# An encoder trunk on one core: two whole tiles set among a lone pair's products, weight tiles picked by time, residual tiles reloaded by pairs, a shorter last norm and an early table load

## The chip, the cores and the metric

The kernel runs on one core of a Trainium2 chip. A core has five engines with queues of their own: TensorE (PE), which multiplies matrices; VectorE (DVE), ScalarE (ACT) and GpSimd (POOL), which work elementwise; and SyncE (SP), which here only issues transfers. Operands lie in an on-chip memory of 128 partitions; TensorE writes its sums into PSUM banks, which another engine reads out (the text calls that an evacuation). The metric is device microseconds of one execution, as a median over runs; less is better.

## The reference, cut to what matters

One layer of an encoder serves 512 prompt tokens and 64 tokens of a running stream together (T = 576 columns). All arithmetic is float32.

```
x += Mixer(RMSNorm(x))          # gated DeltaNet || gated linear attention, both in chunks, merged by sigmoids
x += CrossAttn(RMSNorm(x), mem) # 4 heads into 256 memory tokens; for the prompt, keys and values come from mem
x += ConvFFN(RMSNorm(x))        # up 1024 -> 2 x 2816, causal conv of width 3, SiLU gate, down 2816 -> 1024
y  = RMSNorm(x)                 # norm_final
```

Outputs are y for all tokens, the new recurrent and convolution states, and the memory's keys and values.

## The kernel before

**Layout.** Activations lie with features on partitions: x is eight tiles x[0..7] of 128 features by 576 tokens. A weight tile is 128x1024: eight blocks of 128x128 for one output tile. Every float32 factor is split into a high part in the type float32r (fp32r in the rows) and a low part, the rest; a product is three matmuls, high x high, high x low, low x high. `proj` (L694) does so for a whole output tile in one two-bank PSUM tile (`big`, two of them); for most weights it comes with all low-weight matmuls last (`late`).

**Products by pairs.** Many weights are taken two output tiles at a time (a pair) by a scheme of seven half-size products, P1, Q5, Q6, P2, P3, Q7 and Q4, in place of eight (`products`, L1495; the order is `product_order`, L91). P1, Q6, Q7 and Q4 of a pair add up in one bank in turn ("a"), and each is read out by DVE (the `finish` functions) before the next may add to it. The operands are sums and differences of activation halves (`operands`, L1472: tu, tw, ach, acl and hl in the profile), made by DVE, ACT and POOL ahead of time, and of weight quarters (`emit_product`, L552: ws).

**Weights.** `emit_weight` (L521) loads a float32 tile by SP into a raw tile (wr), makes the high part and the negated raw on ACT, and adds the raw once more into the negated part by an accumulating transfer, issued by POOL: that gives the low part ("w<-wt" and "w<-ws" among the transfers). Some kinds use DVE or POOL instead. Raw tiles come from a ring of 3, high and low tiles from one of 6 (`raw_tile` L506, `w_tile` L513). Half way, `swap_pools` (L1522) gives the space of the small tiles of the recurrent part to a second pool, fp: one more raw tile (rawf), three more w tiles (wf), and eight tiles F0 to F7. Of such a tile the driver knows that it is free at `drv.swapped`, the time of the small tiles' last use. `raw_tile` and `w_tile` take the new ring's tile while that ring isn't full, or where it is free sooner. `fetch` (L620) emits weights ahead in the order of `weight_order` (L64) as long as w tiles are left.

**The order of the work.** A driver (L212) plans while the program is built. `main` (L1534) yields at every few matmuls; between them side chains (spawned generators) are advanced whose inputs the plan holds for ready. Each instruction gets a planned start from cost constants, and each engine's queue is written in the order of planned starts. On the chip every engine takes its queue in that order and waits by semaphores. TensorE's own order is the program's.

**The stages the change touches.**
- Start: 18 warm-up matmuls on a tile of ones (L636) while the first x tiles and weight parts arrive by SP; then high and low parts of x (`xprep`), and the first two projections.
- From the projections to the mixer's output: gate tiles, pool swap, four `out` tiles, the gate pairs' products, `mem_prep` (L2091: loads the memory tiles and makes their high and low parts mh and ml, all at one place), four more `out` tiles. There all eight x tiles are loaded again into F0 to F7 at once (L1753). Then keys and values of the memory, and the four w_o pairs (`wo_finish` adds to x).
- Down projection: partial sums over four parts of the inner features (`ffn_order`, L116). Of part 2, the last pair, tiles 6 and 7, is left over and done alone after the last up projection. It is followed by two whole tiles (0 and 1) of part 3 without the last activation, which is added when it is ready, by the pairs (2, 3) and (4, 5), and by tiles 6 and 7 in halves of the tokens.
- Last norm (L1969 on): acc holds the squares of tiles 0 to 5, sq those of tiles 6 and 7. `sums` adds the three over the features for 128 tokens with a matmul each; `roots` takes the power -0.5; `flip` turns the tiles to tokens on partitions; `put_out` scales and stores them.

```
seq.append(("dns", [(("dn", (6, 2)), ("dn", (7, 2)))]))                  # L126, the lone pair
return seq + [("dn", (0, 1)), ("dns", ...(2, 4)), ("dn", (6, 7))]        # L127
if fp is not None and (len(drv.ring.get("rawf", ())) < RF or drv.free_at("rawf") < drv.free_at("raw")):   # L507
for i, src in enumerate([acc] + sqs[t < 2]):                             # L1999, sums
```

All instructions are recorded by one helper, so every row of the profile has line 244; the tiles' names tell them apart.

## Time and profile before

| | us |
|---|---|
| median of 3 runs | 1117.86 |
| lowest, highest | 1116.87, 1120.01 |
| the profiled execution | 1115.69 |
| its span, first to last instruction | 1113.9 |
| PE busy | 1095.8 |
| DVE busy | 719.3 |
| ACT busy | 660.2 |
| POOL busy | 309.7 |

The rows of the profile read as follows. A timeline row has the start in us from the span's beginning, the time from the group's first start to its last end, the engine (PEld is TensorE's load of the stationary factor; a q stands for an engine's queue that issues transfers), the operation, the tile written, the tiles read, the shape and the count; in brackets stands the idle time of the engine before it and what ended it. Instructions of a kind are merged in such rows, also over others between them. A row of waits has the total, the number and the longest. A row of the table of stages has the stretch, its length, the busy time of PE, PEld, DVE, ACT and POOL with counts, the granted clock, the share of busy transfer engines and GB/s. A row of the chain that ended last has start, length and what the end hung on. The row "DMA to landing" belongs to a tile's transfers in a stretch: least, median and longest time from issue to landing. Ends of matmuls are modelled, so I reckon PE by starts.

### The profile page before, as it was taken

Reading aid. Unit: us, or ns where it says so; the run is one execution under the profiler, and the core shown is the slowest. Engines: PE = TensorE matmul, PEld = TensorE weight load, DVE = VectorE, ACT = ScalarE, POOL = GpSimd, SP = SyncE. Lnnn points to the kernel's source line nnn. Section 1 sums busy time; section 2 is a strip of 40 time slices with the busy share of each in tenths; the row PEclk is TensorE's granted clock in tenths of the full one; section 3 lists DMA queues with packets and bytes.
Section 4 is the critical chain, followed back from the end, with each engine's and each line's share of the span. In section 5 each row is a group of like instructions: output and inputs, shape, how many; then the busy total and the mean of one; then the engine's idle time right before and its main releaser. Section 6 shows DMA issues by size and latency. Waiting matters only on the chain.

```text
span 1113.9 us, 21561 instructions
## 1 busy us (share of the span) xinstructions
PE 1095.8 (98%) x8331; PEld 1058.1 (95%) x8331; DVE 719.3 (65%) x1475; ACT 660.2 (59%) x1254; POOL 309.7 (28%) x559
## 2 busy tenths in 40 slices
PE   9999999999999999999999999999999999999997
PEld 8999989998998999989999999999999999999997
DVE  5566854864654766877557677567836783766585
ACT  6665645563754468466646666665646564656455
POOL 0243315230431233131210122323423242324242
PEclk9999999999999999999999999999999999999999
DMA  8566542453454769797764737975897579749644
GB/s 282 132 151 152 117 79 77 81 120 100 120 121 112 173 157 213 253 229 194 192 169 112 182 79 162 227 168 111 169 231 183 107 166 240 185 92 209 151 98 119
DMA packets 65158, 173.05 MB, mean 155 GB/s; under 512 B 7584, under 2 KB 20000, under 8 KB 65056
## 3 DMA queue, kind: packets, MB, share of 16 engines
q0 software_dynamic: 28368, 72.89, 38.1%
q1 hardware_dynamic: 36688, 98.79, 26.5%
q8 instruction: 66, 1.08, 0.4%
q14 instruction: 36, 0.29, 0.1%
HBM read 161.03 MB, written 5.37 MB: 149 GB/s over the span
## 4 chain that ended last, share of the span: by engine, by line
PE 94%; DMA 2%; DVE 2%; ACT 1%; issue 1%; SPq 0%; ACTq 0%; DVEq 0%
PE big L244 60%; PE sm L244 34%; DMA wr<-wt 1%; DMA w<-wt 1%; DMA w<-ws 1%; ACT w L244 1%; DVE w L244 0%; DVE x L244 0%; DMA x<-xT 0%; DVE ml L244 0%; DVE acl L244 0%; DVE gt L244 0%; DVE acc L244 0%; ACT vraw L244 0%; ACT kgt L244 0%
## 5 line engine op out<-in xcount | busy, mean ns | idle before, releaser
L244 PE MATMUL big<-xh,w 128*128 128x256 f32 (+1 forms) x2816 | 508.9, 300 | 1.5 <-ACT w L244 1.4
L244 PEld LDWEIGHTS big<-xh,w 128*128 128x128 f32 x2816 | 423.8, 189 | 6.5 <-issue 2.0
L244 PE MATMUL big<-xl,w 128*128 128x256 f32 (+1 forms) x1408 | 301.4, 295 | 0.0
L244 PEld LDWEIGHTS big<-xl,w 128*128 128x128 f32 x1408 | 236.8, 189 | 0.2 <-DVE xl L244 0.2
L244 POOL DMA_DIRECT2D w<-wt x129 | 113.2, 880 | 375.5 <-ACT w L244 304.9
L244 PE MATMUL sm<-ach,w 128*128 128x288 f32 (+2 forms) x1008 | 207.0, 296 | 4.2 <-DVE x L244 3.8
L244 ACT CAST w<-wr 128x1024 fp32r<-128x1024 f32 (+3 forms) x195 | 161.5, 830 | 20.9 <-PE big L244 10.1
L244 ACT ACTIVATE w<-wr 128x1024 fp32r<-128x1024 f32 (+3 forms) x174 | 145.2, 835 | 45.4 <-PE big L244 27.4
L244 PEld LDWEIGHTS sm<-ach,w 128*128 128x128 f32 x1008 | 163.6, 188 | 6.3 <-DVE x L244 2.4
L244 PE MATMUL sm<-acl,w 128*128 128x288 f32 (+2 forms) x504 | 138.0, 295 | 0.0
L244 PEld LDWEIGHTS sm<-acl,w 128*128 128x128 f32 x504 | 94.8, 188 | 0.0
L244 DVE TENSOR_TENSOR fu<-big,rbc 128x512 f32<-128x512 f32 (+1 forms) x88 | 36.4, 453 | 77.5 <-PE big L244 75.1
L244 DVE SCALAR_TENSOR_TENSOR fc<-fu,vec,fc 128x578 f32<-128x578 f32 x88 | 72.3, 824 | 20.8 <-ACT fc L244 19.8
L244 ACT ACTIVATE fc<-fu,vec 128x578 f32<-128x578 f32 x44 | 38.4, 872 | 78.4 <-DVE fu L244 78.4
L244 ACT CAST w<-ws 128x384 fp32r<-128x384 f32 (+2 forms) x100 | 53.1, 547 | 34.8 <-DVE ws L244 25.0
L244 POOL COPY fout<-fu 128x2 f32<-128x2 f32 x88 | 29.8, 382 | 151.2 <-DVE fu L244 151.2
L244 DVE TENSOR_TENSOR x<-x,sm 128x288 f32<-128x288 f32 (+2 forms) x127 | 54.1, 440 | 25.7 <-PE sm L244 25.3
L244 DVE TENSOR_TENSOR w<-ws,w 128x384 fp32r<-128x384 f32 (+2 forms) x75 | 46.2, 621 | 14.1 <-ACT w L244 12.9
L244 POOL DMA_DIRECT2D w<-wd x45 | 39.7, 888 | 48.7 <-ACT w L244 45.7
L244 PE MATMUL big<-oh,w 128*128 128x256 f32 (+1 forms) x256 | 45.2, 296 | 3.6 <-DMA w<-wt 2.4
L244 PEld LDWEIGHTS big<-oh,w 128*128 128x128 f32 x256 | 38.6, 188 | 4.2 <-DMA w<-wt 2.6
L244 DVE SCALAR_TENSOR_TENSOR c<-u,vec,c 128x579 f32<-128x579 f32 x36 | 29.4, 820 | 2.6 <-ACT c L244 1.8
(361 smaller groups left out, 1762.3 us busy)
## 6 DMA issues: line engine op xcount, KB each, us to landing
wr<-wt SPq DMA_DIRECT2D x134, 512.0 KB, 6.1
w<-wt POOLq DMA_DIRECT2D x96, 512.0 KB, 7.2
wr<-wd SPq DMA_DIRECT2D x24, 384.0 KB, 5.9
w<-wt POOLq DMA_DIRECT2D x33, 256.0 KB, 6.3
w<-wd POOLq DMA_DIRECT2D x36, 192.0 KB, 5.5
x<-xT SPq DMA_DIRECT2D x16, 288.0 KB, 6.0
w<-ws POOLq DMA_DIRECT2D x11, 256.0 KB, 5.0
w<-ws POOLq DMA_DIRECT2D x12, 192.0 KB, 4.7
```

What stands on the lines that cost most here:

```text
L244: fn(*args, **kw)
```

## The change

Six edits come together.
- **Mix.** The two whole tiles 0 and 1 of part 3 no longer follow the lone pair's seven products but stand among them: after the third product the first part of tile 0 (three activations, in the order 18, 19, 20), after the fourth its low-weight part, after the fifth and sixth the same of tile 1, then the seventh product. The last activation's part follows as before.
- **Tile by time.** `first` compares when the next tile of either ring is free, with `drv.swapped` for one not yet taken, instead of taking the new ring first.
- **Residual tiles by pairs.** x[0] and x[1] are loaded again at the first memory values, the next two after P1 of each w_o pair.
- **Memory tiles as a chain.** `c_mem_prep` issues all four loads and then prepares one tile at a time, spaced by 1.5 us of planned time.
- **Table load.** A tanh on 16 columns of the ones tile stands at the very start; mhalf is set after it. The warm-up has 20 matmuls instead of 18.
- **Last norm.** The squares of tile 6 are added into acc on DVE, so that `sums` has two operands instead of three; tokens 512 to 575 are turned into a `big` tile and tokens 0 to 255 into `sm` tiles, the other way round than before.

```diff
--- before.py
+++ after.py
@@ -35,7 +35,7 @@
 HOP = 0.2
 BACK = 6.0
 MARGIN = 0.6
-NWARM = 18
+NWARM = 20


 C_GMIX, C_GKV, C_GMEM, C_GFFN, C_GFIN = 0, 8, 16, 24, 32
@@ -74,11 +74,15 @@
         else:
             seq += [(kd, (4 if kd == "mv" else 2) * i + j) for j in range(4 if kd == "mv" else 2)]
     seq += [("mo", 0), ("mo", 1)] + [("*", u) for u in product_order(MPAIRS, True)]
-    for kd, i in FFN:
+    for kd, i, *mixed in FFN:
         if kd == "up":
             seq += [("up", i), ("up", NJ + i)]
         elif kd == "dns":
             seq += [("*", u) for u in product_order(i)]
+        elif kd == "mix":
+
+            of_pair = [("*", u) for u in product_order(mixed[0])]
+            seq += of_pair[:3] + [("dn", (i[0], 3))] + of_pair[3:5] + [("dn", (i[1], 3))] + of_pair[5:]
         else:
             seq += [("dn", (m, 3)) for m in i]
     return seq
@@ -122,9 +126,7 @@
             late = []
         pairs = [(("dn", (m, p)), ("dn", (m + 1, p))) for m in range(0, 8, 2)]
         late = [("dns", pairs if p < 2 else pairs[:3])]
-        if p == 3:
-            seq.append(("dns", [(("dn", (6, 2)), ("dn", (7, 2)))]))
-    return seq + [("dn", (0, 1)), ("dns", [(("dn", (m, 3)), ("dn", (m + 1, 3))) for m in (2, 4)]), ("dn", (6, 7))]
+    return seq + [("mix", (0, 1), [(("dn", (6, 2)), ("dn", (7, 2)))]), ("dns", [(("dn", (m, 3)), ("dn", (m + 1, 3))) for m in (2, 4)]), ("dn", (6, 7))]


 FFN = ffn_order()
@@ -285,6 +287,11 @@
         q.append(n)
         self.fresh.add(n)
         return tile_
+
+    def first(self, tag, bufs, other, n):
+
+        free = [(self.swapped if t in ("rawf", "wf") else 0.0) if len(self.ring.get(t, ())) < k else self.free_at(t)[0] for t, k in ((tag, bufs), (other, n))]
+        return free[0] < free[1]

     def free_at(self, tag):
         return min((max([0.0] + list(self.wrote.get(old, {}).values()) + list(self.seen.get(old, {}).values()))
@@ -504,14 +511,14 @@
             drv.pending.discard(ap.tensor.name)

     def raw_tile():
-        if fp is not None and (len(drv.ring.get("rawf", ())) < RF or drv.free_at("rawf") < drv.free_at("raw")):
+        if fp is not None and drv.first("rawf", RF, "raw", RAWB):
             return keep(drv.rotate("rawf", RF, fp.tile([P, 1024], F32, tag="rawf", name=nm("wr"), bufs=RF)))
         return keep(drv.rotate("raw", RAWB, wp.tile([P, 1024], F32, tag="raw", name=nm("wr"), bufs=RAWB)))

     wnames = set()

     def w_tile():
-        if fp is not None and (len(drv.ring.get("wf", ())) < WF or drv.free_at("wf") < drv.free_at("w")):
+        if fp is not None and drv.first("wf", WF, "w", WB):
             t_ = drv.rotate("wf", WF, fp.tile([P, 1024], F32R, tag="wf", name=nm("w"), bufs=WF))
         else:
             t_ = drv.rotate("w", WB, wp.tile([P, 1024], F32R, tag="w", name=nm("w"), bufs=WB))
@@ -632,6 +639,10 @@

     ones_r = cp.tile([P, 128], F32R, name="onesr")
     G.memset(f(ones_r), 1.0)
+
+    mhalf = cp.tile([P, 16], F32, name="mhalf")
+    A.activation(mhalf, f(ones_r)[:, 0:16], AF.Tanh)
+    G.memset(mhalf, -0.5)
     pw = pq.tile([P, 512], F32, tag="sm", name=nm("warm"))
     for _ in range(NWARM):
         PE.matmul(pw[:, 0:128], ones_r, ones_r, start=True, stop=True)
@@ -670,8 +681,6 @@
         return vec_t[:, c:c + n]

     ea = cp.tile([P, 4], F32, name="ea")
-    mhalf = cp.tile([P, 16], F32, name="mhalf")
-    G.memset(mhalf, -0.5)
     wg_t = small_tile([P, 256], F32, tag="wg", name="wg", bufs=1)
     cst_in = small_tile([P, 12, 3], F32, tag="cstin", name="cstin", bufs=1)
     cst_out = small_tile([P, 12, 6], F32, tag="cstout", name="cstout", bufs=1)
@@ -1492,7 +1501,8 @@
             fe = cut(fe, N1)
         return {"P1": fe, "P2": cut(fo, N1), "P3": cut(fo, N2), "Q5": cut(fu, N1), "Q7": cut(fu, N2), "Q6": cut(fw, N1), "Q4": cut(fw, N2)}

-    def products(pairs, ops, finish, late=None):
+    def products(pairs, ops, finish, late=None, among=()):
+

         banks = {}
         for pair, prod in product_order(pairs, late is not None):
@@ -1518,6 +1528,10 @@
             drop(wh)
             fetch(wpos[0])
             yield 0.4
+            for piece in among:
+                if piece == "next":
+                    break
+                yield piece

     def swap_pools():

@@ -1743,17 +1757,21 @@
             yield from out_tile(m)
         yield ("gops",)
         yield from products(GPAIRS, gops, gate_finish)
-        mem_prep()
+        drv.spawn(c_mem_prep())
         for m in range(4, 8):
             if m < 6:
                 drv.spawn(c_wo_operands(2 * m - 7))
             yield from out_tile(m)
             if m % 2:
                 drv.spawn(c_wo_operands(m))
-        for m in range(8):
-            x[m] = xslot(m)
-            DMA(x[m][:, 0:T], xT[:, m, :])
-        yield ("nm",)
+
+        def x_again(m):
+
+            for i in (m, m + 1):
+                x[i] = xslot(i)
+                DMA(x[i][:, 0:T], xT[:, i, :])
+
+        yield ("nm", "mx")
         N["mrt"], N["mbc"] = N["nm"]
         acc = slot("acc")
         out = []
@@ -1764,6 +1782,8 @@
             half = N1 if prod in ("P1", "P2", "Q4") else N2
             V.scalar_tensor_tensor(xx[:, half], b if prod in ("Q5", "P3") else c if prod == "P2" else a, scale, xx[:, half],
                                    op0=ALU.mult, op1=ALU.add)
+            if prod == "P1" and m < 6:
+                x_again(m + 2)
             if prod == ("P2" if m == 6 else "P3"):
                 drv.spawn(c_norm(m, C_GMEM, acc, out))
             elif prod == "Q4":
@@ -1784,6 +1804,8 @@
             if kd == "mk":
                 yield from mem_keys(i)
             elif kd == "mv":
+                if i == 0:
+                    x_again(0)
                 yield from mem_values(i)
             elif kd == "wo":
                 yield tuple(("wops", m) for m in range(1, 8, 2))
@@ -1931,7 +1953,7 @@

         acc = slot("acc")
         gx = []
-        for kd, i in FFN[:-1]:
+        for kd, i, *mixed in FFN[:-1]:
             if kd == "up":
                 j = i
                 ba_, bb_ = [], []
@@ -1952,16 +1974,35 @@
                 yield from products(i, [ops[k] for k in ks[0::2]], dn_finish)
             else:

-                yield tuple(("act", j) for j in PARTS[3][:-1])
                 halves = []
-                for m in i:
-                    ps = big()
-                    wh, wl = weight("dn", (m, 3), m == i[0], m != i[0])
-                    yield from proj(ps, wh, wl, [full[k] for k in PARTK[3][:-1]], True, False, late=True)
-                    halves.append((ps, wh, wl))
+
+                def begun():
+                    yield "next"
+                    yield "next"
+                    yield tuple(("act", j) for j in PARTS[3][:-1])
+                    for m in i:
+                        ps = big()
+                        wh, wl = weight("dn", (m, 3), True)
+                        wready.pop(wpos[0] - 1)
+                        n = 0
+                        for piece in proj(ps, wh, wl, [full[k] for k in PARTK[3][:-1]], True, False, late=True, order=(0, 2, 1)):
+                            yield piece
+                            n += 1
+                            if n == 3:
+                                yield "next"
+                        halves.append((ps, wh, wl))
+                        yield "next"
+
+                pieces = begun()
+                ks = PARTS[2]
+                yield from products(mixed[0], [ops[k] for k in ks[0::2]], dn_finish, None, pieces)
+                for piece in pieces:
+                    if piece != "next":
+                        yield piece
                 yield (("act", NJ - 1),)
                 for m, (ps, wh, wl) in zip(i, halves):
                     yield from proj(ps, wh, wl, [full[NJ - 1]], False, True, k0=len(PARTS[3]) - 1)
+                    drop(wh)
                     for xx, i_ in zip(two(x[m]), pv(ps)):
                         V.tensor_tensor(xx, xx, i_, op=ALU.add)
                     last_tile(m)
@@ -1993,15 +2034,18 @@
                 A.activation(sqs[a < 256][i][:, a:b], x[m][:, a:b], AF.Square)
             for a, b, o in parts:
                 V.tensor_scalar(gs[a < 256][i][:, a:b], x[m][:, a:b], vcol(C_GFIN + m), None, op0=ALU.mult)
+            if i == 0:
+                c = slice(parts[0][0], parts[-1][1])
+                V.tensor_tensor(acc[:, c], acc[:, c], sqs[c.start < 256][0][:, c], op=ALU.add)

         def sums(t):
             a, n = toks[t]
-            for i, src in enumerate([acc] + sqs[t < 2]):
-                PE.matmul(pss[0:n, t:t + 1], src[:, a:a + n], ones[:, 0:1], start=i == 0, stop=i == 2)
+            for i, src in enumerate([acc, sqs[t < 2][1]]):
+                PE.matmul(pss[0:n, t:t + 1], src[:, a:a + n], ones[:, 0:1], start=i == 0, stop=i == 1)

         def flip(t):
             a, n = toks[t]
-            b = None if t == 4 else big()
+            b = None if t < 2 else big()
             fb[t] = [sm(), sm()] if b is None else [b[:, 0, :], b[:, 1, :]]
             for q, g in enumerate(gx + gs[t < 2]):
                 PE.transpose(fb[t][q // 4][0:n, 128 * (q % 4):128 * (q % 4) + 128], g[:, a:a + n], ident)
@@ -2088,12 +2132,14 @@
             N["v", hd] = split(vr[j])


-    def mem_prep():
+    def c_mem_prep():
         DMA(fst, st_ffn)
         N["mx"] = []
-        for i in range(4):
-            mt_ = slot("mem")
+        mts = [slot("mem") for _ in range(4)]
+        for i, mt_ in enumerate(mts):
             DMA(mt_[:, 0:512], memT[:, 512 * i:512 * i + 512])
+        for i, mt_ in enumerate(mts):
+            yield [mt_]
             h = slot("mh", F32R)
             lo = slot("ml", F32R)
             for k in range(2):
@@ -2102,6 +2148,8 @@
                 A.activation(h[:, c], mt_[:, c], AF.Identity, scale=g)
                 V.scalar_tensor_tensor(lo[:, c], mt_[:, c], g, f(h[:, c]), op0=ALU.mult, op1=ALU.subtract)
                 N["mx"].append((h[:, c], lo[:, c]))
+            yield 1.5
+        drv.done.add("mx")

     def c_mem_stat():

```

## The prediction

> **What bounds the kernel now.** I read the page first, then who waits for whom on PE, then the timeline, the chain and the table of stages where a wait falls.
>
> ```profile
> PE 1095.8 (98%) x8331; PEld 1058.1 (95%) x8331; DVE 719.3 (65%) x1475; ACT 660.2 (59%) x1254; POOL 309.7 (28%) x559
> ...
> PE sm L244 <- DVE x L244: 3.8, 3, 1.8
> PE big L244 <- DMA w<-wt: 2.4, 1, 2.4
> PE big L244 <- ACT w L244: 1.4, 1, 1.4
> PE big L244 <- DVE gt L244: 1.2, 2, 1.0
> ```
>
> TensorE is busy for 98% of the span. The change removes hardly any matmul, so it can win only what PE loses by waiting (the four rows: us in total, times, longest; 8.8 in all), what it runs slowly at the start, and what stands at the end: some 10 us of 1114. A gain of 1% is about the ceiling. A measurement of this kernel tells about 0.3%, 3.4 us, from no change.
>
> **Start: table load ahead of the data, two more warm-up matmuls.**
>
> ```profile
> 1.00 4.10 PE L244 MATMUL warm<-onesr 128*128 128x128 f32 x18 [1.00 <-POOL onesr L244]
> 6.51 1.10 PE L244 MATMUL big<-xh,w 128*128 128x256 f32 x2 [1.41 <-ACT w L244]
> ...
> 4.15 1.28 ACT L244 ACT_TABLE_LOAD   x1 [4.15 <-DMA x<-xT]
> ...
> 5.86 0.60 ACT L244 CAST w<-wr 128x512 fp32r<-128x512 f32 x1
> ...
> L244 SPq DMA_DIRECT2D wr<-wt x1: 432/432/432, 1.7 to 1.7; - x1
> DMA to landing us min/median/max: 3.4/3.4/3.4
> ...
> 11.01 1.16 PE L244 MATMUL big<-xh,w 128*128 128x256 f32 x4
> 11.97 0.68 PE L244 MATMUL big<-xl,w 128*128 128x256 f32 x2
> ...
> 13.54 0.69 PE L244 MATMUL big<-xh,w 128*128 128x256 f32 x4
> 14.07 0.42 PE L244 MATMUL big<-xl,w 128*128 128x256 f32 x2
> ...
> 0.00:23.00 23.00, 20.59 (x122) 19.76 (x126) 12.62 (x21) 17.98 (x27) 2.66 (x12) 1.00 0.85 292
> ```
>
> The load of 1.28 us begins only when x has landed, at 4.15. With a tanh on the constant ones tile ahead of it, ACT loads its table while x is under way, and the first xh begins at 4.15. The first weight part, issued at 1.7, lands 3.4 later at 5.1, and its cast (0.60) ends at 5.7: PE begins about 0.75 us earlier, not 1.28. Two more warm-up matmuls are 2 x 0.23 (4.10 / 18) and end at 5.6, inside the gap: nothing. POOL sets mhalf only after the tanh; its first reader is the first norm, far behind, and no other work on POOL is due before. No table load is added: the first table already serves a tanh (the gates') and an exp.
>
> What 0.75 us is worth depends on the rate. Four matmuls take 0.96 us from 11.01 to 11.97 and 0.53 from 13.54 to 14.07: until about 13 PE runs at half pace, though the granted clock (the last row's 1.00) shows none of it. At half pace 0.75 us is 0.4 us of work: the lower end. If the switch moves too, from 13 to 9.6, half of 3.4 us is saved besides: 2.1, the upper end. The gap ahead of 6.51 is the large one of these first microseconds and it closes, but the rows show one switch and not what sets it; I take 1.0, nearer the lower end.
>
> The Trainium skill, "TensorE: Matmul & The Clock Gate", Part 1, says that the array runs at half clock until one free-running window of about 3.4 us was busy. By that rule the closed gap moves the switch by a window or not at all, and the sum would have 2.1 or 0.4 here. The trace agrees in the factor of two; no row shows the windows.
>
> **Pool swap: tiles picked by time.**
>
> ```profile
> 362.27 1.33 PE L244 MATMUL big<-xh,w 128*128 128x256 f32 x8
> ...
> 370.25 1.06 ACT L244 ACTIVATE w<-wr 128x1024 fp32r<-128x1024 f32 x1 [3.76 <-DMA wr<-wt]
> ...
> 364.31 7.52 DMA wr<-wt
> ...
> 371.84 7.30 DMA w<-wt
> ...
> 379.19 0.81 PE L244 MATMUL big<-oh,w 128*128 128x256 f32 x4 [2.36 <-DMA w<-wt]
> ```
>
> After the swap the kernel takes the new ring's tiles as long as that ring isn't full, though they are free only when the small tiles' last reader is done, about 364. So out tile 2's weights land at 370.25, are accumulated from 371.84 on, and PE waits 2.36 for them. With the times compared, its raw tile comes from the old ring and is loaded before; its w tile is the last gate tile's, read until 363.6 (362.27 + 1.33). Then 1.06 for the negated copy, about 0.5 to the issue and 7.30: 372.5, where PE comes at 376.8. The late tiles go to out 3, due 6 us later, and the products behind it. Ends: 2.36 if nothing else is late, 0 if another weight takes the place; I take 2.2, since the next has 6 us more.
>
> **Mem tiles as a spawned chain, x by pairs.**
>
> ```profile
> 449.00 3.25 DVE L244 SCALAR_TENSOR_TENSOR ml<-mem,vec,mh 128x256 fp32r<-128x256 f32 x8
> ...
> 452.99 0.50 PE L244 MATMUL big<-oh,w 128*128 128x256 f32 x2 [0.99 <-DVE gt L244]
> ...
> 437.50 15.90 SPq L244 DMA_DIRECT2D x<-xT  x8
> ...
> DMA to landing us min/median/max: 5.9/12.8/16.4
> ...
> 392.00:414.00 22.00, 22.00 (x168) 22.00 (x167) 14.94 (x28) 13.78 (x29) 6.10 (x7) 1.00 0.82 180
> 480.00:491.00 11.00, 9.67 (x73) 9.43 (x72) 7.96 (x16) 8.11 (x17) 2.59 (x3) 1.00 0.94 224
> 491.00:502.00 11.00, 11.00 (x84) 10.77 (x83) 7.84 (x15) 6.58 (x13) 3.45 (x4) 1.00 0.97 209
> ...
> 484.57 0.40 PE L244 MATMUL sm<-ach,w 128*128 128x288 f32 x1 [1.33 <-DVE x L244]
> ```
>
> Eight ml in one block (3.25) stand ahead of the gate's evacuation on DVE, and PE waits for its bank. In four steps the block is 0.8 at a time, and evacuations fit between: of the 1.2 in the waits' row I take 1.0 (ends 0 and 1.2).
>
> The eight x loads hold SP for 15.90 us from 437.50, with weights queued behind them, and take 5.9 to 16.4 to land. By pairs they leave that stretch and enter the w_o products, two per pair of products (11 us), whose DMA share is 0.94 and 0.97 already. The gate products of 392 to 414, the same work, run at 0.82, so part of that is catching up and room is there. Each x is asked for after P1 of one pair and read after P1 of the next, 11 us on, against a landing of 5.9 at best. On SP it stands behind weights that wait for a raw tile. I cost it at nothing; what hides it is these 11 us, and without them it costs landing less 11, up to 5.4 at 16.4. The other end is 0.5 won, weights behind mem coming sooner. The 1.33 at 484.57, DVE held by the value heads, isn't touched.
>
> **The lone pair mixed with two whole tiles.**
>
> ```profile
> 1065.51 1.35 PE L244 MATMUL sm<-hl,w 128*128 128x288 f32 x9
> ...
> 1069.41 0.76 DVE L244 TENSOR_TENSOR acl<-fc,ach 128x576 fp32r<-128x576 f32 x1
> ...
> 1070.42 1.28 DVE L244 SCALAR_TENSOR_TENSOR fc<-fu,vec,fc 128x578 f32<-128x578 f32 x1
> 1071.63 1.00 DVE L244 TENSOR_TENSOR x<-x,sm 128x288 f32<-128x288 f32 x2
> ...
> 1072.21 0.37 PE L244 MATMUL sm<-ach,w 128*128 128x288 f32 x1 [1.79 <-DVE x L244]
> ...
> 1070.00:1076.00 6.00, 4.21 (x33) 4.01 (x32) 5.57 (x12) 1.12 (x3) 2.19 (x3) 1.00 0.70 158
> ```
>
> The lone pair's products (nine matmuls, 1.2 us each) use one bank in turn: Q7 has to wait until DVE has read Q6, and DVE is at fc until 1071.7. Now three whole-tile steps (four matmuls, 0.53 each) stand behind Q6 and more behind P3, and Q7 comes some 2.4 us later, past both. The third step needs act 20's low part, ready at 1070.17 (1069.41 + 0.76); PE gets there at 1065.51 + 3 x 1.2 + 2 x 0.53 = 1070.2, just in time. So the 1.79 goes. Late next is DVE: busy for 5.57 of 6 us, it has still to make the last activation's operands and the pairs' weights, which PE now wants 1.8 sooner. Ends 1.8 and 0; I take 1.3.
>
> **Last norm.**
>
> ```profile
> 1098.87 0.28 PE L244 MATMUL sm<-keep,acc 128*128 128x1 f32 x2
> ...
> 1100.63 1.09 PE L244 MATMUL big<-keep,gx 128*128 128x128 f32 x8
> ...
> 1103.85 0.28 PE L244 MATMUL sm<-keep,acc 128*128 128x1 f32 x2
> ...
> 1105.11 1.04 PE L244 MATMUL sm<-keep,gx 128*64 128x128 f32 x8
> ```
>
> Five token sums take 1.76 us (1098.87 to 1100.63) and 1.26 (1103.85 to 1105.11). Each loses one operand of three, a third: 0.59 + 0.42 = 1.0. Two additions on DVE are new (128x320, 128x256), about 0.5 each by the row of two x (1.00); the first stands ahead of tile 7's evacuation, 0.1 of it on the path. The turned tiles' other banks are free by then: nothing. I take 0.9 (0.4 to 1.3).
>
> **Sum.** 1.0 + 2.2 + 1.0 + 1.3 + 0.9 = 6.4 us. The profiled execution took 1115.69 (span 1113.9): 1109.3. The median of the runs, 1117.86, is 2.2 above it, and so I set the changed one: 1111.5.
>
> **Rivals.** *Given back.* The waits go but DVE behind the mix, or a second late weight behind the swap, makes new ones: only 0.4 + 0.7 + 0.9 + 0.5 (half the ml wait) stay, 2.5 us, 1115.4. For it: DVE's 5.57 of 6, and the planner lays the whole order anew, so that small waits can come anywhere. Against: each wait has a cause of its own in the rows.
> *Clock earlier.* The switch near 9.6: 1.1 more than in the sum, 1110.4. The skill's rule above is this one.
> *Slower: x late.* An x that lands late holds DVE, so the bank, so PE, at pairs 2, 4 and 6. It decides from a landing 11 us behind the request; at 16.4 each costs 5.4, 16.2 in all less 6.4: 9.8 slower, 1127.7. For it: the DMA shares, and the 484.57 row, where x stands on DVE behind other work. Against: 16.4 was for eight at once behind mem and weights. The Trainium skill, same page and part, calls DVE's queue strictly first-in first-out; the 484.57 row agrees.
>
> **Numbers.** The sum 0.55, clock earlier 0.17, given back 0.20, x late 0.08. The first alone spans 1108.5 to 1114.3. Range: down by all upper ends, 2.1 + 2.36 + 1.2 + 0.5 + 1.8 + 1.3 = 9.3, and the 1.33, to 1107.5; up past given back to 1116.8. Faster by over 0.3% (1114.5): 0.55 + 0.17 + a quarter of given back, 0.77; within 0.14, the most of the rest of it; slower 0.09.
>
> **What would show it.** The first matmul into big near 5.75; no wait of PE for w<-wt near 376, nor for gt near 453; x landing within 11 us; no wait near 1072, and how full DVE is there; two operands per token sum and an end about 1 us nearer to the last product. The prediction is wrong if PE waits 2 us or more for DVE or DMA in the w_o products, behind the swap or in the down projection.

## The result and the profile after

| | before | changed |
|---|---|---|
| median of 14 runs, us | 1116.96 | 1117.21 |
| ratio | | 1.0001 (0.9992 to 1.0011) |
| the profiled execution, us | 1115.69 | 1116.63 |
| its span, us | 1113.9 | 1114.9 |

Measured again on another chip the ratio was 1.0014 (1.0003 to 1.0024). I forecast 1111.5, which is 0.6% below the 1117.86 that I started from; the change made no difference. The 6.4 us of my sum went somewhere, and the profile after shows where to look. First its page (PE's row) and the waits of PE, with total, times and longest:

```profile
PE 1098.2 (99%) x8323; PEld 1060.9 (95%) x8323; DVE 720.4 (65%) x1477; ACT 660.8 (59%) x1255; POOL 310.8 (28%) x559
...
PE sm L246 <- DVE x L246: 2.9, 3, 1.9
PE big L246 <- DVE gt L246: 2.7, 1, 2.7
PE sm L246 <- DMA w<-ws: 1.5, 1, 1.5
```

The 2.36 for w<-wt is gone. But PE's busy time rose from 1095.8 to 1098.2, with eight matmuls fewer in the records; the wait for gt, which I had struck out, has grown from 1.0 to 2.7; a wait for w<-ws is new. The timeline, with start, length, engine and what is done:

```profile
5.88 1.10 PE L246 MATMUL big<-xh,w 128*128 128x256 f32 x2 [0.35 <-ACT w L246]
...
451.06 0.22 DVE L246 SCALAR_TENSOR_TENSOR gt<-gt,big 128x64 f32<-128x64 f32 x1 [1.02 <-PE big L246]
451.20 1.80 DVE L246 TENSOR_TENSOR w<-wr,w 128x1024 fp32r<-128x1024 f32 x1
...
452.92 0.67 DVE L246 SCALAR_TENSOR_TENSOR gt<-gt,big 128x512 f32<-128x512 f32 x1
...
453.74 0.51 PE L246 MATMUL big<-oh,w 128*128 128x256 f32 x2 [2.71 <-DVE gt L246]
...
454.51 1.16 PE L246 MATMUL big<-oh,w 128*128 128x256 f32 x4
...
458.27 0.69 PE L246 MATMUL big<-oh,w 128*128 128x256 f32 x4
...
503.57 0.93 PE L246 MATMUL sm<-ach,w 128*128 128x288 f32 x5 [1.54 <-DMA w<-ws]
...
1082.40 1.54 DVE L246 TENSOR_TENSOR x<-x,big 128x512 f32<-128x512 f32 x4
1083.86 0.45 DVE L246 TENSOR_TENSOR x<-x,sm 128x288 f32<-128x288 f32 x1
...
1084.37 0.40 PE L246 MATMUL sm<-ach,w 128*128 128x288 f32 x1 [1.89 <-DVE x L246]
...
1087.38 0.92 PE L246 MATMUL sm<-ach,w 128*128 128x288 f32 x3
...
1089.71 0.56 PE L246 MATMUL sm<-ach,w 128*128 128x288 f32 x3
...
1100.65 0.28 PE L246 MATMUL sm<-keep,acc 128*128 128x1 f32 x2
...
1101.85 1.09 PE L246 MATMUL big<-keep,gx 128*128 128x128 f32 x8
```

PE starts 0.63 earlier (5.88 against 6.51), and five token sums take 1.20 instead of 1.76 (1100.65 to 1101.85). At 451 DVE reads 64 columns of an `out` tile, then makes the low part of a key weight (1.80), and only then reads the other 512 columns, for which PE waits 2.71. Behind that wait, and behind the one at 1084.37, the same matmuls take 1.16 instead of 0.69, and 0.92 instead of 0.56: half pace, for a while. The table of stages (length, busy time of PE, PEld, DVE, ACT, POOL, then the granted clock) shows for how long:

```profile
450.70:454.10 3.40, 0.69 (x6) 0.48 (x5) 3.04 (x5) 1.62 (x2) 1.22 (x1) 1.00 0.81 297
454.10:457.60 3.50, 3.50 (x17) 3.50 (x17) 3.47 (x7) 0.00 (x0) 0.00 (x0) 0.51 0.53 180
1082.20:1085.60 3.40, 1.51 (x12) 1.28 (x11) 3.20 (x9) 2.75 (x5) 0.72 (x1) 1.00 0.16 25
1085.60:1089.00 3.40, 3.40 (x16) 3.40 (x15) 2.64 (x8) 2.92 (x10) 1.88 (x3) 0.50 0.42 100
```

In both places a stretch of 3.4 us in which PE stood still for more than half the time is followed by one of 3.4 us at half clock, which costs 1.7. The stretches are cut where the profile's clock record can change: in every trace the entries of that record last whole multiples of 3.41 us, and this grid lies differently in each execution (the first moment at full clock comes between 9.3 and 13.1 us in the 20 profiles).

PE's lead over the kernel before, from the starts of the same matmuls in both traces:

| at, us | 6 | 22 | 381 | 462 | 487 | 513 | 1066 | 1081 | 1093 | end |
|---|---|---|---|---|---|---|---|---|---|---|
| lead, us | 0.6 | 1.5 | 4.1 | 1.4 | 3.0 | 1.3 | -0.5 | 1.5 | -1.8 | -1.0 |

So the gains came, at the start, at the swap (381), at 487 (the old wait of 1.33) and at the mix (1081), and each was lost again: at 453, from 503 on, and at 1084. From 513 to 1066 some 1.8 went, a part of it without any wait.

### The profile page after: what moved, and what is told of

Read it like the earlier page. It is cut to its first block, busy times and chain, and to the rows that moved or that the text cites. A ratio compares the mean times of both kernels' runs of the same rounds, so it can differ in the third digit from the quotient of the medians.

```text
span 1114.9 us, 21570 instructions
## 1 busy us (share of the span) xinstructions
PE 1098.2 (99%) x8323; PEld 1060.9 (95%) x8323; DVE 720.4 (65%) x1477; ACT 660.8 (59%) x1255; POOL 310.8 (28%) x559
## 4 chain that ended last, share of the span: by engine, by line
PE 96%; DVE 1%; DMA 1%; ACT 1%; issue 1%; SPq 0%; DVEq 0%; ACTq 0%
PE big L246 62%; PE sm L246 34%; DMA w<-ws 1%; ACT w L246 0%; DVE x L246 0%; DMA wr<-wt 0%; DVE w L246 0%; DVE acl L246 0%; DVE acc L246 0%; ACT kgt L246 0%; ACT ach L246 0%; DVE ws L246 0%; DVE yo L246 0%; SPq L246 0%; DVE gt L246 0%
## 5 line engine op out<-in xcount | busy, mean ns | idle before, releaser
L246 POOL DMA_DIRECT2D w<-ws x23 | 19.9, 867 | 42.6 <-ACT w L246 37.7
```

Of the source, the lines that this page charges most:

```text
L246: fn(*args, **kw)
```

## The experiments

Theory A: each part wins what I counted, and new waits eat it, two of them with a half-clock window. Rivals: the parts win nothing by themselves; whatever PE wins is given back at the next wait; the half pace has another cause. Ratios are to the kernel before, run beside each kernel; 0.001 is 1.1 us.

**The half clock: r1.** Idle matmuls fill the two waits of the changed kernel.

```diff
+ for _ in range(18): matmul(spare[:, 0:256], wh[:, 0:128], osx[0][0][:, 0:256])   # ahead of 453.7
+ for _ in range(14): matmul(banks[bank][:, HT:512], wh[:, 0:128], h[:, 0:224])   # ahead of 1084.4
```

> The changed kernel with 18 idle matmuls (128x256 into an unused bank) ahead of the matmul that waits at 453.7, and 14 (128x224 into unused columns) ahead of the one that waits at 1084.4; all other engines' queues are the same. Theory A (a wait near or above 2 us drops TensorE's clock to half for one window of 3.4 us, which costs 1.7 us each): both waits keep their ends, the matmuls behind them run at full pace, 1117.2 - 2 x 1.7 = 1113.8. Rival B (the half pace has another cause than PE's idle time, such as DVE's or the whole chip's load): half pace stays, 1117.2 or later by what the idle matmuls overrun. Rival C (half pace goes, but the later waits take the gain): 1115.5 to 1117.

The 14 open the bank of Q5 anew, so that this kernel leaves a part of Q5's sum out of x; the work is otherwise the same. The ratio was 0.9992 (0.9980 to 1.0004). Its table of stages over the same two places:

```profile
450.70:454.10 3.40, 3.24 (x27) 3.07 (x26) 3.27 (x7) 1.63 (x2) 0.54 (x1) 1.00 0.93 310
454.10:457.60 3.50, 3.50 (x28) 3.50 (x28) 3.47 (x6) 0.00 (x0) 0.00 (x0) 1.00 0.41 167
1080.60:1084.00 3.40, 3.07 (x25) 2.88 (x25) 3.20 (x10) 2.51 (x5) 0.73 (x1) 1.00 0.23 37
1084.00:1087.40 3.40, 3.40 (x28) 3.40 (x27) 3.18 (x9) 3.40 (x11) 1.96 (x3) 1.00 0.33 84
```

DVE is about as late as before (it begins to read the 512 columns at 452.24, against 452.92), PE still can't go on, yet the clock stays at 1.00: the half clock comes from PE standing still. In the traces this was worth 2.4 us of span (1112.5 against 1114.9), in the runs 1.0 to 2.5 (the changed kernel stood at 1.0001 and at 1.0014), less than the 3.4 I expected and nearest to rival C: the next wait for w<-ws grew from 1.5 to 2.2, and not every execution need have both windows.

**Relieving DVE with POOL: r2, r3, r4.** All from the changed kernel. r2:

```diff
-            X.tensor_tensor(lo[:, :n], raw[:, :n], f(h[:, :n]), op=ALU.subtract)
+            (G if (kind, idx) in (("mk", 0), ("mk", 1)) else X).tensor_tensor(...)
```

> The changed kernel with the low parts of the first two key weights made by POOL instead of DVE (2 x 1.2 to 1.8 us of DVE work stood between the two parts of an evacuation near 451). Theory A (that weight's place in DVE's queue makes the wait of 2.71 and with it the half-pace window): wait and window go, 4.0 us sooner at 458; with the DMA waits near 503 to 525 as they are, 1113.2. Rival B (the wait is DVE's total work there, mem chain included): a wait of 1 us or more for gt stays, 1116. Rival C (the DMA waits in the w_o products take it back, since weights come no sooner): wait goes, but waits for w<-ws grow by as much, 1116 to 1117.

r3:

```diff
+ drv.spawn(c_late(m, ps), 1)          # tiles 0 and 1 read out after `yield 9.0`
- if late and i == 0                   # product_order: P1, P2, Q5, ... also for the pair (2, 3)
+ if (late or pair[0] == ("dn", (2, 3))) and i == 0
- V.tensor_tensor(s_[:, 0:n], a, b, op=ALU.add)
+ (G if pair[0] == ("dn", (4, 3)) else V).tensor_tensor(s_[:, 0:n], a, b, op=ALU.add)
```

> The changed kernel with DVE relieved behind the mix: tiles 0 and 1 are read out 9 us later, P2 stands ahead of Q5 in the pair (2,3), POOL makes the weight sums of the pair (4,5). Theory A (DVE's backlog is the wait of 1.89 at 1084.4 and the half-pace window behind it): both go, 3.3 us sooner, 1113.9. Rival B (the last activation's operands are late too, so PE waits for them instead): 1115.5 to 1117.

r4 has both:

> r2's and r3's edits together. Theory A (the gains of the six parts are real and two waits with their half-pace windows eat them): 1117.2 - 4.0 - 3.3 = 1109.9, near the prediction's 1111.5. Rival B (other waits take the place): 1114 or more.

All three were slower than the changed kernel: 1.0044 (1.0027 to 1.0060), 1.0054 (1.0038 to 1.0070) and 1.0077 (1.0060 to 1.0094). The waits were still there, 2.4 for gt in r2 and 1.89 at 1086.9 in r3. In r2 the two low parts run on POOL and DVE beside them:

```profile
446.22 5.31 POOL L246 TENSOR_TENSOR w<-wr,w 128x1024 fp32r<-128x1024 f32 x2 [6.51 <-ACT w L246]
...
446.64 5.96 DVE L246 SCALAR_TENSOR_TENSOR ml<-mem,vec,mh 128x256 fp32r<-128x256 f32 x4
```

Four ml take 5.96 where the changed kernel needed 1.67. In r3 it is the same with the last activation's operands:

```profile
1082.43 1.03 POOL L246 TENSOR_TENSOR ws<-wr 128x256 f32<-128x256 f32 x1
...
1082.61 2.16 DVE L246 TENSOR_TENSOR acl<-tw,ach 128x576 fp32r<-128x576 f32 x1
```

2.16 for an acl that takes 0.76 elsewhere. Work moved to POOL holds DVE up while it runs. The Trainium skill, "SBUF — State Buffer", section "Who interferes with whom", says that a DVE instruction with two inputs in the on-chip memory and a GpSimd instruction that reads it block each other in full; these rows agree, and the 1.80 at 451.20 (1.22 elsewhere) is the same, beside an acl on POOL. My repairs were wrong, and they leave theory A undecided: DVE didn't become freer by them. They also made a wait at the end (2.93 at 1099.6 in r3), since the tiles read out later fell among the last products.

**One part alone: s1 to s4**, each the kernel before with just that part of the diff.

```diff
s1: NWARM = 20; A.activation(mhalf, f(ones_r)[:, 0:16], AF.Tanh) at the start
s2: def first(...), used in raw_tile and w_tile
s3: drv.spawn(c_mem_prep()); x_again(m) at mv 0 and behind P1
s4: ("mix", (0, 1), ...) in ffn_order, with `among` in products
```

> The kernel before with the early table load and 20 warm-up matmuls alone. Theory A (each part wins what its own place shows; in the changed kernel later waits eat it): first product 0.6 us sooner, the switch to full pace one window sooner, 1.5 us at 22 us, and the lead is kept to the end, since nothing later stands still by the clock: 1117.0 - 1.5 = 1115.5. Rival B (a lead of PE is given back at the next transfer or DVE wait): the waits at 379, 453 and 1072 grow by 1.5 in all, 1117.0.

> The kernel before with the tiles picked by time alone. Theory A: the wait of 2.36 near 379 goes, 2.4 to 2.6 us sooner to 450; the wait for gt near 453 (0.99 before) stays as it is: 1114.6. Rival B (given back): the wait for gt grows to 2 us or more and brings a half-pace window with it, 1116 to 1117.5. By the changed kernel's trace, where just this happened with the memory tiles in steps, I hold B for as likely as A.

> The kernel before with the memory tiles as a chain and x by pairs alone. Theory A (the new waits near 453 and from 503 to 525 belong to these two edits): the 1.33 at 484.6 goes, a wait of 1 to 2.7 for gt stands near 453, waits for w<-ws of 1.5 to 2.8 in all stand in the w_o products: 1117 to 1120. Rival B (those waits came only because PE was 4 us ahead there): none of them, 1115 to 1116.

> The kernel before with the two whole tiles among the lone pair's products alone. Theory A (DVE is full there, so the 1.79 at 1072 comes back at 1084 as a wait of 1.9, and a half-pace window costs 1.7 more): 2.0 sooner at 1081, then 1.3 later than before at 1090, 1118.3. Rival B (the wait at 1084 comes from the changed kernel's other shifts in DVE's queue): no wait there, 1115.2.

| | ratio | us | counted |
|---|---|---|---|
| s1 start | 0.9985 (0.9975 to 0.9995) | -1.7 | -1.0 |
| s2 tile by time | 0.9975 (0.9963 to 0.9988) | -2.8 | -2.2 |
| s3 memory chain and x by pairs | 1.0038 (1.0022 to 1.0054) | +4.2 | -1.0 |
| s4 mix | 0.9988 (0.9977 to 1.0000) | -1.3 | -1.3 |

The start and the tiles by time win, by about what was counted; the mix has the number that was counted, but its interval ends at no change; the two loading edits lose, by 1.3 more than theory A's range for s3 allowed. In s2 the wait for gt stays at 1.0 with PE 3.6 ahead: a lead isn't simply given back. Not all of s2's 2.8 belongs to the struck wait. The wait of 2.36 in the profile of before is 1.26, 1.52 and 1.25 in s1, s3 and s4, which keep its order, and some 0.6 came from the slots (below). In s4 neither of my cases came whole: the wait is back behind the mix (1.91 at 1081.69) with a half-clock stretch behind it, as in theory A, but the time is nearer to rival B's. Theory A had compared with a single profile of before, in which the wait of 1.79 happened to cost no half clock; that this makes the difference is likely and not shown.

In s3 both new waits are there without any lead from the swap: 2.8 for gt, and

```profile
505.95 0.94 PE L244 MATMUL sm<-ach,w 128*128 128x288 f32 x5 [1.87 <-DMA w<-ws]
```

s1 and s2 also show the grid. Both keep the wait of 1.79 near 1068, in s1 over the border of two stretches, in s2 within one (first s1, then s2):

```profile
1064.50:1067.90 3.40, 2.58 (x20) 2.34 (x18) 3.06 (x6) 2.85 (x8) 2.19 (x4) 1.00 0.84 149
1067.90:1071.30 3.40, 2.44 (x18) 2.47 (x19) 2.97 (x7) 0.09 (x1) 1.11 (x2) 1.00 0.86 193
```

```profile
1065.80:1069.20 3.40, 1.61 (x13) 1.41 (x12) 3.30 (x6) 0.99 (x3) 1.89 (x2) 0.99 1.04 248
1069.20:1072.60 3.40, 3.40 (x17) 3.40 (x16) 2.30 (x6) 0.66 (x2) 0.31 (x1) 0.50 0.29 45
```

The same wait cost 1.7 more in s2's profile. The profiled execution of before had both its large waits over such borders, at full clock throughout.

**The changed kernel with parts undone: u1 to u4.**

```diff
u1: mem_prep() at one place and eight x at once, as before; the rest as changed
u2: mem_prep() at one place; x by pairs
u3: c_mem_prep() as a chain; eight x at once
u4: u1, and ("dns", [(6, 2), (7, 2)]) with ("dn", (0, 1)) behind it, as before
```

> The changed kernel without the memory tiles as a chain and without x by pairs (both as before). Singles give, against before, 1.7 for the start, 2.8 for the tiles by time, 1.3 for the mix, and the trace 0.6 for the last norm: 6.4 less, 1110.4. Theory A (the two loading edits are the loss, the rest adds up): 1109.5 to 1111.5; wait for gt near 450 of 1.0 as before, no waits for w<-ws above 0.6. Rival B (gains given back whatever the edit): 1114 to 1117.

> The changed kernel without the memory chain, with x by pairs. DVE's queue has the evacuation ahead of the two key weights again. Theory A1 (the chain makes the wait near 453, x by pairs those from 503 to 525): no wait above 1.3 near 453, waits for w<-ws of 1.5 to 2.8 stay: u1 plus 1.5 to 2.8, 1112 to 1113.5. A2 (x by pairs costs nothing by itself): as u1, 1110.4.

> The changed kernel without x by pairs, with the memory chain. In DVE's queue two low parts of key weights (128x1024) stand ahead of the 512-column part of an evacuation. Theory A1: wait of 2 to 2.8 near 453 and, where it lies in one window, 1.7 of half pace; no waits for w<-ws: u1 plus 2.7 less 1.0 plus 1.3 (1.7 three times in four), 1113.4. A2 (the chain alone is harmless): as u1, 1110.4.

> u1 without the mix: start, tiles by time and last norm. The wait of 1.79 near 1068 is back, none of 1.9 near 1080. By theory A (the mix moves a wait of 1.8 to 1.9 from one place to the other and wins little): u1 plus 0 to 1.3, 1110.4 to 1111.7. Rival B (the mix wins its 2.0 as in the changed kernel's trace near 1081): 1112.5.

| | ratio | us | against u1 |
|---|---|---|---|
| u1 neither | 0.9956 (0.9942 to 0.9971) | -4.9 | |
| u2 x by pairs | 0.9975 (0.9963 to 0.9987) | -2.8 | +2.1 |
| u3 chain | 0.9978 (0.9969 to 0.9988) | -2.5 | +2.5 |
| u4 no mix | 0.9959 (0.9943 to 0.9974) | -4.6 | +0.3 |

u1, with a median of 1112.19, beats both kernels. It lies 0.7 above theory A's range and far below rival B's, and its waits are those of theory A. In u4 the wait of 1.79 is back (at 1068.20), and the time is theory A's: the mix moves a wait and wins little. With one of the loading edits the kernel is over 2 slower than u1, with both 5.0 (0.9956 to 1.0001); the intervals of u1 and u2 overlap, so that for u2 the traces have to tell. For the chain the place is plain. DVE and PE in u3, and then in u1:

```profile
451.08 0.22 DVE L246 SCALAR_TENSOR_TENSOR gt<-gt,big 128x64 f32<-128x64 f32 x1 [1.51 <-PE big L246]
451.22 1.22 DVE L246 TENSOR_TENSOR w<-wr,w 128x1024 fp32r<-128x1024 f32 x1
452.35 0.68 DVE L246 SCALAR_TENSOR_TENSOR gt<-gt,big 128x512 f32<-128x512 f32 x1
...
453.18 0.51 PE L246 MATMUL big<-oh,w 128*128 128x256 f32 x2 [2.14 <-DVE gt L246]
```

```profile
447.64 0.69 DVE L246 SCALAR_TENSOR_TENSOR gt<-gt,big 128x512 f32<-128x512 f32 x1
448.24 1.23 DVE L246 TENSOR_TENSOR w<-wr,w 128x1024 fp32r<-128x1024 f32 x1
...
448.47 0.50 PE L246 MATMUL big<-oh,w 128*128 128x256 f32 x2 [1.00 <-DVE gt L246]
```

In one block, the eight ml end and the whole evacuation follows. In steps, the planner finds gaps of other sizes in DVE's time: the 64-column part fits ahead of a key weight, the 512-column part behind it. That order is written into DVE's queue, and PE waits for it, in u3's profile with a half-clock window. A1 holds for the chain: by the starts u3 is 0.4 behind u1 ahead of these rows and 2.6 behind at 462, and the span is 2.5 longer.

For x by pairs neither A1 nor A2 does: u2 has no wait for w<-ws among its longest, though one accumulation takes 8.9 us to land (490.20 to 499.13), and yet it lost 2.1. By the starts it goes from 0.1 ahead of u1 at 528 to 2.9 behind at 1062; 0.4 of that comes at once near 665, the rest slowly through the up projection, without a wait.

**The slots: v1, v2, v5, v6.** Within the up projection the same 576 matmuls take, from the first of them to the product behind, in u1 and in u2:

```profile
811.02 0.42 PE L246 MATMUL big<-xh,w 128*128 128x256 f32 x2
...
887.10 1.35 PE L246 MATMUL sm<-hl,w 128*128 128x288 f32 x9
```

```profile
812.12 0.43 PE L246 MATMUL big<-xh,w 128*128 128x256 f32 x2
...
888.98 1.22 PE L246 MATMUL sm<-hl,w 128*128 128x288 f32 x8
```

76.08 against 76.86, that is 6.34 and 6.41 for a tile of 48. Activations take their places (slots) in a ring of 56 tiles of one size. The high and low parts of x lie in other slots in u2, and stay there for all 44 tiles; the weights do too. To change the slots of x alone, three are left empty:

```diff
             sq_acc(acc, x[m], m == 0)
+            if m == 0:
+                for _ in range(3): G.memset(slot("pad")[:, 0:1], 0.0)
             out.append((m, norm_prep(x[m], vcol(C_GFFN + m))))
```

> u1 with three slots of the ring left empty through the feed-forward part (three one-column memsets on POOL, 0.2 us each, are all that is added; every queue's order is the same), so that the high and low parts of x for the up projection lie in other slots. Theory D (how long a matmul takes depends on the slots its operands lie in; the slow drift of u2 and of the changed kernel in the up projection is that): the six matmuls per feature tile change by 5 to 25 ns each way, the 44 up tiles by up to 3 us in all, no wait changes: 1109.5 to 1115. Rival E (drift comes from the DMA load or from other engines' work beside the up projection): the same times per tile as u1 within 1 ns, 1112.2.

> u2 (x by pairs) with the same three empty slots. Theory D: the sum over an up tile, 6.41 us in u2 against 6.34 in u1, is drawn anew; if it comes near 6.34 to 6.37, u2's loss shrinks from 2.1 to about 0.5 and the time is 1112 to 1113.5. Rival E: 6.41 stays, 1114.4.

> u1 once more beside the three others on the same chip: 0.9956 of the kernel before, as it was.

The ratios were 0.9952 (0.9938 to 0.9965) for v1, 0.9954 (0.9941 to 0.9967) for v2 and 0.9956 (0.9942 to 0.9970) for v4. v2's two rows:

```profile
812.20 0.43 PE L246 MATMUL big<-xh,w 128*128 128x256 f32 x2
...
888.44 1.36 PE L246 MATMUL sm<-hl,w 128*128 128x288 f32 x9
```

76.24 against u2's 76.86: with x by pairs and other slots the loss is gone. Every engine has the same instructions in the same order as in u2, but for the three memsets, and the weights have the same addresses. In v1 the sum hardly changes (6.333), but single feature tiles move by -9.7 to +6.3 ns against u1, where rival E allowed 1. Rival E falls and theory D fits: u2's 2.1 goes with where the operands landed, not with the loads. But the slots aren't the whole of it: r4 has all x in r2's slots, and yet in its profile the first 12 up tiles take 6.407 us each, u2's value, and the later ones 6.353 as all of r2's do. Why is open. The changed kernel has 76.48 there against 76.26 before; the same three slots were left empty in it:

> The changed kernel with the same three empty slots, all queues in the same order. Its sum over an up tile was 6.372 us, u1's 6.340, so its slots cost it 44 x 0.032 = 1.4. Theory D: the sum is drawn anew between 6.33 and 6.41, and the time moves by 44 times the difference: at 6.34, 1115.7; at 6.41, 1118.8. Rival F (in the changed kernel the waits near 453, 503 and 1084 take up whatever the slots give): 1117.2 whatever the sum.

> The changed kernel once more beside it: 1.000 of the kernel before, sum of an up tile 6.372.

The ratios were 1.0007 (0.9996 to 1.0018) for v5 and 1.0014 (1.0003 to 1.0024) for v6. The draw gave 6.358 for a tile against 6.372: 44 times the difference is 0.6, and the runs moved by 0.8, less than they can tell, so that D and F stay undecided by the time; the traces part by 0.7 over the up projection. By the traces, then, the slots explain 1.4 of the changed kernel's 5.0 against u1 (44 x 0.032). The rest, from the starts in both traces: 2.8 at 453, 2.3 in the waits from 503 to 514, less 1.6 at the wait of 1.33 that u1 still has near 479.

**The wait behind the mix: v3.**

```diff
- if late and i == 0                   # u1's product_order
+ if (late or pair[0] == ("dn", (2, 3))) and i == 0
```

> u1 with product P2 ahead of Q5 in the pair (2,3) behind the mix, so that 0.8 us more of PE's work lies between P1 and Q6, which waits for DVE to read P1; DVE's order is the same but for one place. Theory A: the wait of 1.89 becomes 1.1, so that it can't bring a half-pace window any more: 0.8 sooner, and 0.9 more on average over where the windows fall, 1110.5 to 1111.4. Rival B (the next evacuation, of Q5 or Q6, takes the 0.8): 1112.2.

The ratio was 0.9980 (0.9971 to 0.9990), 2.7 slower than u1, which neither case foresaw. Where u1 waits for DVE once for 1.89 and once for 0.21, v3 does so four times, 3.4 in all:

```profile
1080.11 0.41 PE L246 MATMUL sm<-ach,w 128*128 128x288 f32 x1 [0.61 <-DVE x L246]
...
1082.47 0.40 PE L246 MATMUL sm<-ach,w 128*128 128x288 f32 x1 [1.29 <-DVE x L246]
...
1084.04 0.40 PE L246 MATMUL sm<-ach,w 128*128 128x288 f32 x1 [0.51 <-DVE x L246]
...
1091.60 0.37 PE L246 MATMUL sm<-ach,w 128*128 128x288 f32 x1 [0.99 <-DVE x L246]
```

Rival B is the nearer one: the next evacuations took the 0.8, and more. But the planner also laid the queues of DVE, ACT and POOL anew from 1065 on, at more than the one place that I had expected. So v3 shows that this order doesn't help; that DVE bounds the stretch behind the mix whatever PE's order is not shown.

## Why the prediction was wrong

**Start** (1.0 counted): right. First product at 5.88 against 5.75; s1 won 1.7 (0.6 to 2.8). The switch to full pace came at 9.3 to 12.7 in sixteen profiled executions with the edit (10.6 on average), and at 10.0 to 13.1 in four without it (11.1): about the 0.6 by which PE starts sooner, within a spread of over 3 us from the grid. *Clock earlier* was no case of its own.

**Pool swap** (2.2): right in the mechanism: the wait of 2.36 is gone in s2, no second late weight came. In the number there is luck: the struck wait varies from 1.25 to 2.36 between profiles, and s2's 2.8 has 0.6 from the slots in it.

**Memory chain** (1.0 won, ends 0 and 1.2): this is the step that failed. "In four steps the block is 0.8 at a time, and evacuations fit between": in the plan other things fit between as well, and the 512-column evacuation went behind a key weight. PE then waited 2.71 for gt, where I had named no wait there as a sign of being right; u3 shows 2.5 lost in place of 1.0 won. I had set the lower end at 0 with no reason that excluded a loss, though the same text said that the planner lays the whole order anew.

**x by pairs** (0): right by its loads, wrong by 2.1 in u2, which goes with the slots and was in no term of mine. No engine waits for an x on its way, although one took up to 11.8 us to land (490.93 to 502.71 in the changed kernel), more than the 11 that I had relied on. The waits for w<-ws need both loading edits: neither u2 nor u3 has them among its longest. Why the accumulation is issued late with both (495.05 against 490.20 in u2) is open.

**Mix** (1.3, ends 0 and 1.8): the words were right, "late next is DVE", and the ends hold: 1.3 alone (0 to 2.6), 0.3 beside u4. The 1.79 goes and 1.89 comes.

**Last norm** (0.9): the sums lost 0.56 and 0.28 (1105.07 to 1106.05 against 1103.85 to 1105.11) in the traces, 0.84 in all. It was not run alone.

Without the two loading edits my steps add to 1.0 + 2.2 + 1.3 + 0.9 = 5.4, and u1 measured 4.9, twice. That is closer than the steps deserve: by the sums of an up tile (6.340 in u1, 6.355 before) some 0.6 of the 4.9 is a better draw of slots. *Given back* came nearest, but it looked behind the swap and behind the mix; only the second was there. *Slower: x late* didn't happen. And one thing was in none of my prices: I counted each wait at its length, while one of 1.8 us or more costs up to 1.7 more, if it falls into one stretch of the clock's grid. (The lower end of my range adds up to 1107.2, not 1107.5; nothing hangs on it.)

## What to carry to other kernels

Where a planner writes the queues, cutting a block into steps lets other work in between; price such an edit on both sides, and compare the written order of the queue whose evacuations PE needs before believing the gain. Try each part of a bundle alone and undone: here two of six edits hid 5 us that the others had won. A drift without waits over a long stage of equal matmuls can come from where their operands lie; move an allocation and measure again before blaming the edit.

## What the runs showed of the hardware

**Half a stretch of standing still is enough for half the clock.** Stretches of 3.4 us with PE busy for 0.69, 1.26, 1.51 and 1.61 were followed by one at 0.5; others with 1.81, 2.06 and 2.44 were not. Near 1.7 both were seen (1.75 in r2 was, 1.71 in u4 wasn't), and one with 1.61 (r3 at 1097.8) wasn't either; that stays open. The plainest case is one kernel profiled twice, as u1 and as v4, with the same wait of 1.89 (first u1, then v4):

```profile
1077.80:1081.20 3.40, 2.06 (x15) 2.06 (x16) 3.20 (x10) 3.17 (x7) 0.72 (x1) 1.00 0.00 0
1081.20:1084.60 3.40, 3.19 (x24) 2.98 (x23) 3.17 (x10) 3.40 (x11) 3.02 (x5) 1.00 0.63 127
```

```profile
1077.60:1081.00 3.40, 1.51 (x12) 1.28 (x11) 3.40 (x10) 1.91 (x5) 0.72 (x1) 1.00 0.29 39
1081.00:1084.40 3.40, 3.40 (x17) 3.40 (x16) 3.09 (x8) 2.92 (x8) 1.36 (x2) 0.50 0.19 27
```

So single profiles of two kernels can differ by 1.7 us at a wait that both have. The Trainium skill, "TensorE: Matmul & The Clock Gate", Part 1, has the clock fall after at least one idle window of about 3.4 us, on a free-running grid. The grid agrees; a window needn't be idle as a whole, and the measurement decides.

**The pace of matmuls changes with the slots of their operands.** For one feature tile, six matmuls, the mean was 780 to 818 ns, by slot. Kernels that agree in the slots agree within 1 ns for each of the eight tiles (u1, u4 and s2; before, s1 and s4; the changed kernel and r1). Over 44 tiles the best and the worst arrangement seen differ by 3.2 us (6.333 in v1, 6.406 in u2). Which property of an address does it wasn't found, and r4's first 12 up tiles (6.407 us, against 6.353 in r2 with the same slots) show that something else can do it too. For the weights no such thing is seen: in the changed kernel they change between nine slots from tile to tile, and yet inside its long stretches all up tiles but the first take 6.373 or 6.374 us. (The weights' slots lie 4096 bytes apart, those of x 2336.)

**POOL stops DVE.** An instruction of DVE took 2.16 instead of 0.76 and four took 5.96 instead of 1.67 while POOL worked on operands in the same memory.
